# A decoder layer on one core: attention operands of 128 rows, values in 160 columns and loaded last, the norms' steps on GpSimd, and projection weights at the input's place modulo 512

## The chip, the core and the metric

The kernel runs on one core of a Trainium2 chip. The core has a matmul engine (TensorE, PE; its weight loads are listed apart as PEld), three engines for elementwise work (VectorE or DVE, ScalarE or ACT, GpSimd or POOL), and an engine that here only issues transfers (SyncE, SP). Each engine takes its instructions in order, and engines wait for one another by semaphores. Operands lie in on-chip memory, SBUF, as 128 rows (partitions), and an address below is the byte at which an operand starts within a row. The metric is the time of one execution on the device, in microseconds (us).

## The reference

One layer with batch 1, 2048 tokens, width 1024, in float32. Attention has 8 heads of 64 columns, the two other mixers 4 heads each.

```python
h = _rms(x, norm_mix_g);  z = h @ w_in + b_in       # columns split among three mixers
qa, ka = _rms(heads(a_q), a_q_g), _rms(heads(a_k), a_k_g)
c  = cumsum(log_sigmoid(a_f))                       # forget gate, one value per head and token
s  = qa @ ka^T * d**-0.5 + c[q] - c[k]              # causal, softmax over keys
ya = _rms(softmax(s) @ v, g_a)                      # normed per head of 64 columns
yb = sigmoid(b_o) * _rms(mlstm(silu(conv4(b_qk)), b_v, b_i, b_f), g_b)
yc = silu(c_g) * _rms(hgrn2(silu(c_q), logf, c_i), g_c)
x  = x + concat(ya, yb, yc) @ w_out
h  = _rms(x, norm_ffn_g)
u  = conv3(h @ w_up) + conv_b
x  = x + (silu(u_gate) * u_up) @ w_down
```

## The kernel before

**Precision.** A float32 operand is split into a high part (`hi`, rounded for the matmul engine's fp32r form) and a low part (`lo`, the rest). A product is three matmuls, hi by hi, hi by lo and lo by hi, all added into one accumulator: `mm3` (L193, its matmul is L198).

**Projection (z).** The normed input lies transposed in `hhi` and `hlo`, 16 KB a row for each half of the tokens. `z_groups` walks groups of columns of the weight. `load_split` (L178) brings the weights of a group in raw pieces, ACT makes `whi` (L188) and POOL `wlo` (L189). The *natural* groups have 256 or 264 weight columns, which the matmul streams against 128x128 pieces of the input; their result is drained by DVE with the bias added (`z<-w,bias`, L289). The groups for transposed results stream 512 columns of the input against weight pieces. Before the change `whi` starts at 192 or 448 modulo 512 (two buffers) and `hhi` at 64. The two other mixers run merged between the groups. Constants are cast at the start by `consts` (L1709) through one small buffer, `craw`: each load (L1715) waits for the cast before (L1716).

**Queries, keys, values** are written to the device's memory as they come out of the projection: `s_qh`, `s_ql`, `s_kh`, `s_kl` (L404) and `s_v` (L321), by POOL's queue, with the memsets (L315, L316) that complete a value tile.

**Attention.** For each head, `att_load` (L805) lets SP load two operand pairs. QA and KA (128 rows) hold high and low parts of queries and keys. QB and KB use 70 rows: 64 of queries and keys, and six with ones, maxima and gates, so that one matmul adds the gates and takes away the row maxima. V holds 16 blocks of 130 columns: 64 high values, a column for the sum, and 64 low values. Each head has two sets of tiles, used in turn.

The order is written out by hand. A head has 40 steps, one per block of 128 keys and up to 512 queries. A step issues the scores (L885 with KB and QB, L886 with KA and QA), ACT's exponential (L892) and its copy to the high part `ph` (L894), and the subtraction that makes the low part `pl` (L898): in three steps of four on POOL at once, in the fourth on DVE one step later. The row maxima of blocks further on are taken by another matmul (L845, `m<-KB,QB`) and a DVE maximum (L850), 12 of them before the first step. The values' three matmuls (L911, L912, L913; the last uses `pl`) follow the scores three steps behind. The loads of the next head stand early in a head (those of the first two before the first step).

`Later` is a list of functions to be called some steps on. Through it, `att_finish` (L937) norms a head in the next head's steps: squares on ACT, sums and the reciprocal root by Newton steps on DVE (`rms_steps`, L113: one start L120 to L122, and three rounds L130 to L132, one round a step), the scaling on DVE (L971), the gain on POOL (L976) and the store. The last head is finished in four quarters, one after each block of queries.

**After attention** come the output projection (`phase_out`, L198 again, with `wohi` and `yh`) and the feed-forward part (L1252, L1409). The functions that the diff touches, and what calls them:

## Time and profile before

| | before |
|---|---|
| median of 3 runs (lowest to highest) | 2932.36 us (2932.19 to 2941.21) |
| profiled execution, span | 2937.63 us, 2935.5 us |
| mean granted clock of TensorE | 0.977 |
| PE busy | 2817.4 us (96%) |
| DVE, POOL, ACT busy | 2005.9, 1435.1, 1280.0 us |
| projection with the two other mixers | 0 to 939 us |
| attention | 939 to 1443 us |
| output projection | 1443 to 1646 us |
| feed-forward | 1646 to 2935 us |

The profile is of one execution. Its page gives busy times and the costliest groups of instructions; the trace behind it also gives single instructions with their start. In such a row stand the start, the duration (both in us), the engine, the line, the operation with the tiles it writes and reads (out<-in) and their shapes, a count, and in brackets how long the engine was idle before it and what ended that. A window's row gives the busy time and count of each engine in a stretch of time, and the clock that TensorE was granted there, as a share of full speed. Matmuls overlap at their ends, so their spacing is read from start to start.

### The profile page before, as it was taken

Reading aid. Unit: us, or ns where it says so; the run is one execution under the profiler, and the core shown is the slowest. Engines: PE = TensorE matmul, PEld = TensorE weight load, DVE = VectorE, ACT = ScalarE, POOL = GpSimd, SP = SyncE. Lnnn points to the kernel's source line nnn. Section 1 sums busy time; section 2 is a strip of 40 time slices with the busy share of each in tenths; the row PEclk is TensorE's granted clock in tenths of the full one; section 3 lists DMA queues with packets and bytes.
Section 4 is the critical chain, followed back from the end, with each engine's and each line's share of the span. In section 5 each row is a group of like instructions: output and inputs, shape, how many; then the busy total and the mean of one; then the engine's idle time right before and its main releaser. Section 6 shows DMA issues by size and latency. Waiting matters only on the chain. (4 is left out here: it accounts for less than half of the span.)

```text
span 2935.5 us, 42833 instructions
## 1 busy us (share of the span) xinstructions
PE 2817.4 (96%) x15181; PEld 2342.7 (80%) x15181; DVE 2005.9 (68%) x3384; ACT 1280.0 (44%) x2167; POOL 1435.1 (49%) x1199
## 2 busy tenths in 40 slices
PE   7999988999988999999899899999999999999999
PEld 7898987889988666666688788888788888888887
DVE  7337687265786787778546577677797577777655
ACT  4213323132322778878424344444454343444443
POOL 2245452334454577766302366666475644444443
PEclk9999997999999999999999999999999999999999
DMA  4424434333334554342257444444777333333666
GB/s 159 127 93 133 150 96 143 94 108 97 111 107 143 107 114 88 81 92 49 72 179 246 148 155 151 154 148 158 268 247 271 114 108 108 108 105 117 232 214 209
DMA packets 346615, 411.07 MB, mean 140 GB/s; under 512 B 47650, under 2 KB 234096, under 8 KB 343232
## 3 DMA queue, kind: packets, MB, share of 16 engines
q1 hardware_dynamic: 292016, 318.45, 37.2%
q10 hardware_dynamic: 51952, 81.45, 7.6%
q0 software_dynamic: 2432, 8.42, 0.8%
q8 instruction: 120, 1.97, 0.3%
q14 instruction: 95, 0.78, 0.1%
HBM read 280.24 MB, written 127.98 MB: 139 GB/s over the span
## 5 line engine op out<-in xcount | busy, mean ns | idle before, releaser
L1221 POOL TENSOR_TENSOR w<-w,w 128x512 fp32r<-128x512 f32 x302 | 404.8, 1353 | 403.3 <-ACT w L1220 339.2
L1409 PE MATMUL ps<-w,w 128*128 128x512 f32 x1848 | 420.9, 389 | 4.0 <-ACT w L1400 2.0
L1409 PEld LDWEIGHTS ps<-w,w 128*128 128x128 f32 x1848 | 346.6, 188 | 77.6 <-ACT w L1400 2.4
L198 PE MATMUL w<-whi,hhi 128*128 128x256 f32 (+1 forms) x1280 | 370.4, 289 | 3.1 <-DVE lr L1766 2.0
L198 PE MATMUL w<-whi,hlo 128*128 128x256 f32 (+1 forms) x1280 | 371.3, 290 | 0.0
L198 PE MATMUL w<-wlo,hhi 128*128 128x256 f32 (+1 forms) x1280 | 370.4, 290 | 0.6 <-POOL wlo L189 0.6
L898 POOL TENSOR_TENSOR pl<-pf,ph 128x512 fp32r<-128x512 f32 (+2 forms) x240 | 287.8, 1212 | 146.6 <-ACT ph L894 133.3
L1402 POOL TENSOR_TENSOR w<-w,w 128x512 fp32r<-128x512 f32 x154 | 216.3, 1412 | 200.9 <-ACT w L1400 155.4
L1220 ACT ACTIVATE w<-w 128x512 fp32r<-128x512 f32 x302 | 180.4, 627 | 258.7 <-POOL w L1221 86.7
L850 DVE TENSOR_REDUCE mx<-m 128x1 f32<-128x512 f32 (+2 forms) x320 | 190.8, 605 | 91.3 <-PE m L845 63.1
L1401 DVE TENSOR_TENSOR w<-w,w 128x512 fp32r<-128x512 f32 x154 | 179.9, 1178 | 103.4 <-ACT w L1399 102.0
L198 PEld LDWEIGHTS w<-whi,hhi 128*128 128x128 f32 x1280 | 245.2, 192 | 4.8 <-issue 3.8
L198 PEld LDWEIGHTS w<-wlo,hhi 128*128 128x128 f32 x1280 | 244.9, 191 | 2.7 <-POOL wlo L189 1.0
L198 PEld LDWEIGHTS w<-whi,hlo 128*128 128x128 f32 x1280 | 244.7, 191 | 1.8 <-issue 0.5
L892 ACT ACTIVATE pf<-s 128x512 f32<-128x512 f32 (+1 forms) x320 | 172.5, 539 | 91.1 <-PE s L886 50.9
L1226 DVE TENSOR_TENSOR w<-w,w 128x512 f32<-128x512 f32 x176 | 149.8, 870 | 85.3 <-DMA w<-in_w_up_dram 81.0
L189 POOL TENSOR_TENSOR wlo<-wraw,whi 128x1024 fp32r<-128x1024 f32 (+1 forms) x56 | 135.3, 2433 | 111.7 <-ACT whi L188 102.2
L894 ACT ACTIVATE ph<-pf 128x512 fp32r<-128x512 f32 (+1 forms) x320 | 185.1, 578 | 10.3
L1267 DVE SCALAR_TENSOR_TENSOR u<-ps,fcol,u 128x1023 f32<-128x1023 f32 x88 | 108.9, 1279 | 95.3 <-ACT u L1266 95.3
L913 PE MATMUL pv<-pl,V 128*65 128x512 f32 (+1 forms) x320 | 121.7, 380 | 25.2 <-DVE pl L898 24.3
L1400 ACT ACTIVATE w<-w 128x512 fp32r<-128x512 f32 x154 | 96.6, 628 | 111.3 <-PE ps L1409 88.7
L1399 ACT ACTIVATE w<-w 128x512 fp32r<-128x512 f32 x154 | 95.9, 623 | 89.8 <-POOL w L1402 44.4
(374 smaller groups left out, 7092.1 us busy)
## 6 DMA issues: line engine op xcount, KB each, us to landing
w<-in_w_up_dram SPq DMA_DIRECT2D x182, 256.0 KB
w<-s_g SPq DMA_DIRECT2D x154, 256.0 KB
w<-in_w_down_dram SPq DMA_DIRECT2D x110, 256.0 KB
wraw<-in_w_in_dram SPq DMA_DIRECT2D x48, 512.0 KB
s_g<-u ACTq DMA_DIRECT2D x88, 256.0 KB
w<-s_w SPq DMA_DIRECT2D x88, 256.0 KB
s_g<-w ACTq DMA_DIRECT2D x66, 256.0 KB
x<-in_x_dram SPq DMA_DIRECT2D x32, 512.0 KB
```

The costliest lines, as they stand in the source:

```text
L189: nc.gpsimd.tensor_tensor(lo[:, q : q + n, :], raw, h.bitcast(F32), op=ALU.subtract)
L198: nc.tensor.matmul(out, lsl(lhs[a], i), rsl(rhs[b], i), start=(i == 0 and j == 0), stop=(i == n - 1 and j == 2))
L850: nc.vector.tensor_reduce(mx[:, i, kb : kb + 1], m[:, 0:n], axis=AX.X, op=ALU.max)
L892: nc.scalar.activation(pf[:, c0:], s[:, c0:], AF.Exp)
L894: nc.scalar.activation(ph[:, c0:], pf[:, c0:], AF.Copy)
L898: eng.tensor_tensor(pl[:, c0:], pf[:, c0:], ph[:, c0:].bitcast(F32), op=ALU.subtract)
L1220: nc.scalar.activation(h, t, AF.Copy)
L1221: nc.gpsimd.tensor_tensor(lo, t, h.bitcast(F32), op=ALU.subtract)
L1226: nc.vector.tensor_tensor(t, x, y, op=op)
L1401: nc.vector.tensor_tensor(gl, gr, gh.bitcast(F32), op=ALU.subtract)
L1402: nc.gpsimd.tensor_tensor(wl, wr, wh.bitcast(F32), op=ALU.subtract)
L1409: nc.tensor.matmul(tiles[tile], g[x][:, tile * P : (tile + 1) * P], w[y], start=j == 0 and c == 0, stop=j == nj - 1 and c == 2,)
```

## The change

1. `load_split` gives each weight tile 17 x 128 columns (8704 bytes, a multiple of 512) whatever its width, so both buffers start at 64 modulo 512, as the input does. A small pad tile goes, and two small tiles share a tag.
2. The casts of `consts` go through the three buffers of the tag `z`, which the projection's drains use too, in place of `craw`.
3. QB and KB become two fixed pairs of 128 rows. POOL zeroes rows 64 to 128 of both pairs once, before the first loads of ones and gates; L845 and L885 use all rows.
4. A row of V has 160 columns, and its low part begins at column 96. Each load of V is two transfers (65 and 64 columns), and all of V is loaded after the queries and keys.
5. In `att_finish`, the two scalings by the reciprocal sum, the three Newton rounds (four operations each in place of three) and the last scaling of the factor run on POOL; the start of the rounds stays on DVE. All heads share one tile of squares, and the last head's quarters are finished 18, 10, 4 and 4 steps after their last values in place of 4.

```diff
@@ -36,6 +36,8 @@
 NEG = -1e30
 
 SKEW, LEAD0, LEAD = 3, 12, 22
+
+VL, VW = 96, 160
 
 PLM = 4
 
@@ -110,7 +112,7 @@
         pass
 
 
-def rms_steps(k, pool, out, ss, n, epsf, tag):
+def rms_steps(k, pool, out, ss, n, epsf, tag, pool_too=False):
 
     nc = k.nc
     shp = list(ss.shape)
@@ -124,6 +126,12 @@
     )
     for _ in range(3):
         yield
+        if pool_too:
+            nc.gpsimd.tensor_tensor(u, out, out, op=ALU.mult)
+            nc.gpsimd.tensor_tensor(u, u, h, op=ALU.mult)
+            nc.gpsimd.tensor_scalar(out=u, in0=u, scalar1=1.5, scalar2=None, op0=ALU.add)
+            nc.gpsimd.tensor_tensor(out, out, u, op=ALU.mult)
+            continue
         if shp[1] == 1:
             nc.vector.scalar_tensor_tensor(u, out, h, out, op0=ALU.mult, op1=ALU.mult)
         else:
@@ -179,8 +187,11 @@
 
     nc = k.nc
     width = src.shape[1]
-    hi = k.t(wp, [P, DT, width], F32R, tag=tag + "hi")
-    lo = k.t(wp, [P, DT, width], F32R, tag=tag + "lo")
+
+    hi, lo = (
+        k.t(wp, [P, 17 * P], F32R, tag=tag + x)[:, 0 : DT * width].rearrange("p (n c) -> p n c", c=width)
+        for x in ("hi", "lo")
+    )
     for q in range(0, DT, n):
         raw = k.t(wp, [P, n, width], tag=tag + "raw")
         nc.sync.dma_start(raw, src[q * P : (q + n) * P, :].rearrange("(dt p) c -> p dt c", p=P))
@@ -214,7 +225,7 @@
 def z_stats(k, pz, xbufs):
 
     nc = k.nc
-    ss = k.t(pz, [P, 8], tag="n8s", bufs=1)
+    ss = k.t(pz, [P, 16], tag="ss")[:, 0:8]
     for b in range(2):
         for t in range(4):
             (x,) = z_load(k, 1, b, xbufs, t, 1)
@@ -805,8 +816,9 @@
 def att_load(k, h, st):
 
     r = slice(h * HD, (h + 1) * HD)
-    QA, KA, QB, KB = (k.t(k.pat[f"{t[1]}{h % 2}"], [P, T], F32R, tag=t) for t in ("QA", "KA", "QB", "KB"))
-    V = k.t(k.pat[f"V{h % 2}"], [P, 16, 130], F32R, tag="V")
+    QA, KA = (k.t(k.pat[f"A{h % 2}"], [P, T], F32R, tag=t) for t in ("QA", "KA"))
+    QB, KB = k.qkb[h % 2]
+    V = k.t(k.pat[f"V{h % 2}"], [P, 16, VW], F32R, tag="V")
     st.update(QA=QA, KA=KA, QB=QB, KB=KB, V=V, h=h)
 
     def ld(dst, src):
@@ -817,13 +829,14 @@
     ld(QB[64:70], k.s_one[0:6])
     ld(KB[64:68], k.s_one[6:10])
     ld(KB[68:70], k.s_fc[h])
-    v = k.s_v[:, h, :].rearrange("(jt p) c -> p jt c", p=P)
-    ld(V[:, 0:4], v[:, 0:4])
     ld(QA[0:64], k.s_qh[r])
     ld(QA[64:128], k.s_ql[r])
     ld(KA[0:64], k.s_kl[r])
     ld(KA[64:128], k.s_kh[r])
-    ld(V[:, 4:16], v[:, 4:16])
+    v = k.s_v[:, h, :].rearrange("(jt p) c -> p jt c", p=P)
+    for j in (slice(0, 4), slice(4, 16)):
+        ld(V[:, j, 0:65], v[:, j, 0:65])
+        ld(V[:, j, VL : VL + 64], v[:, j, 65:129])
 
 
 def att_maxima(k, sts, pa, ps, later):
@@ -843,7 +856,7 @@
                     nn = max(n, 256)
                     m = k.t(ps["m"], [P, BLK], tag="m")
                     nc.tensor.matmul(
-                        m[:, 0:nn], QB[0:70, q0 : q0 + P], KB[0:70, kb * BLK : kb * BLK + nn], start=True, stop=not last
+                        m[:, 0:nn], QB[:, q0 : q0 + P], KB[:, kb * BLK : kb * BLK + nn], start=True, stop=not last
                     )
                     if last:
                         nc.tensor.matmul(m[:, n - P : n], k.identb, k.mnat, start=False, stop=True)
@@ -882,7 +895,7 @@
     q0 = d * P
     qs = slice(qb * BLK + c0, (qb + 1) * BLK)
     s = k.t(ps["s"], [P, BLK], tag="s")
-    nc.tensor.matmul(s[:, c0:], KB[0:70, js], QB[0:70, qs], start=True, stop=False)
+    nc.tensor.matmul(s[:, c0:], KB[:, js], QB[:, qs], start=True, stop=False)
     nc.tensor.matmul(s[:, c0:], KA[:, js], QA[:, qs], start=False, stop=j < 4 * qb)
     if j >= 4 * qb:
         nc.tensor.matmul(s[:, q0 : q0 + P], k.identb, k.mtr, start=False, stop=d < 3)
@@ -909,7 +922,7 @@
     po = st["po"]
     nj = 4 * qb + 4
     nc.tensor.matmul(po[:, c0:], V[:, j, 0:65], ph[:, c0:], start=j == 0, stop=False)
-    nc.tensor.matmul(po[0:64, c0:], V[:, j, 65:129], ph[:, c0:], start=False, stop=False)
+    nc.tensor.matmul(po[0:64, c0:], V[:, j, VL : VL + 64], ph[:, c0:], start=False, stop=False)
     nc.tensor.matmul(po[:, c0:], V[:, j, 0:65], pl[:, c0:], start=False, stop=j == nj - 1)
     if j < nj - 1:
         return
@@ -929,7 +942,8 @@
 
     later.put(1, out)
     if h == AH - 1:
-        att_finish(k, st, pa, 4 * qb, 4, later, 4)
+
+        att_finish(k, st, pa, 4 * qb, 4, later, (18, 10, 4, 4)[qb])
     elif qb == 3:
         att_finish(k, st, pa, 0, 16, later, 4)
 
@@ -946,7 +960,9 @@
         o = st["o"][:, t0 : t0 + n, :]
         w["num"] = o[:, :, 0:64]
         w["rl"] = k.t(pa, [P, n], tag=f"rl{n}", bufs=bufs)
-        w["sq"] = k.t(pa, [P, n, HD], tag=f"asq{n}", bufs=bufs)
+        if n == 16 or "sq" not in st:
+            st["sq"] = k.t(pa, [P, 16, HD], tag="asq", bufs=1)
+        w["sq"] = st["sq"][:, t0 : t0 + n, :]
         w["ss"] = k.t(pa, [P, n], tag=f"ass{n}", bufs=bufs)
         nc.vector.reciprocal(w["rl"], o[:, :, 64])
 
@@ -957,17 +973,17 @@
         nc.vector.tensor_reduce(w["ss"][:, c], w["sq"][:, c], axis=AX.X, op=ALU.add)
 
     def scale():
-        nc.vector.tensor_tensor(w["ss"], w["ss"], w["rl"], op=ALU.mult)
-        nc.vector.tensor_tensor(w["ss"], w["ss"], w["rl"], op=ALU.mult)
+        nc.gpsimd.tensor_tensor(w["ss"], w["ss"], w["rl"], op=ALU.mult)
+        nc.gpsimd.tensor_tensor(w["ss"], w["ss"], w["rl"], op=ALU.mult)
         w["s"] = k.t(pa, [P, n], tag=f"as{n}", bufs=bufs)
-        w["chain"] = rms_steps(k, pa, w["s"], w["ss"], HD, 1.0, f"a{n}")
+        w["chain"] = rms_steps(k, pa, w["s"], w["ss"], HD, 1.0, f"a{n}", pool_too=True)
 
     def link():
         next(w["chain"], None)
 
     def times(c):
         if c.start == 0:
-            nc.vector.tensor_tensor(w["s"], w["s"], w["rl"], op=ALU.mult)
+            nc.gpsimd.tensor_tensor(w["s"], w["s"], w["rl"], op=ALU.mult)
         nc.vector.tensor_tensor(
             w["sq"][:, c], w["num"][:, c], w["s"][:, c].unsqueeze(2).broadcast_to([P, 4, HD]), op=ALU.mult
         )
@@ -1003,8 +1019,16 @@
 
     sts = [{} for _ in range(AH)]
     later = Later()
+
+    k.qkb = [[k.t(k.pat[f"B{i}"], [P, T], F32R, tag=t) for t in ("QB", "KB")] for i in range(2)]
+    def zero(i):
+        for x in k.qkb[i]:
+            k.nc.gpsimd.memset(x[64:128].bitcast(F32), 0.0)
+
+    zero(0)
     with k.tc.manual_schedule():
         att_load(k, 0, sts[0])
+        zero(1)
         att_load(k, 1, sts[1])
         mx = att_maxima(k, sts, pa, ps, later)
         for _ in range(LEAD0):
@@ -1586,7 +1610,6 @@
             for _ in z_norm(k, 0, 0, pz, psw, xb):
                 pass
             z = z_groups(k, 0, pz, wp, psw, xb)
-            pz.tile([P, 24], F32, tag="padz", name="padz", bufs=1)
             state(k, mconst)
             for _ in range(ZC):
                 next(z)
@@ -1711,7 +1734,7 @@
     nc = k.nc
 
     def cast(dst, src):
-        raw = cm.tile([P, P], F32, tag="craw", name=k.nm("craw"))[:, 0 : src.shape[1]]
+        raw = k.t(pz, [P, P], tag="z", bufs=3)[:, 0 : src.shape[1]]
         nc.sync.dma_start(raw, src)
         nc.vector.tensor_copy(dst, raw)
```

The order of the instructions moves at three places. First POOL's queue at the end of the projection and the start of attention, before the change, from the completion of the last value tile (`h`) on:

```order
L318 TENSOR_TENSOR h_9610<-z_9553,h_9610 128x4x64
L321 DMA s_v<-h_9604 128x520
L321 DMA s_v<-h_9610 128x520
L898 TENSOR_TENSOR pl_9787<-pf_9783,ph_9785 128x512
L898 TENSOR_TENSOR pl_9805<-pf_9801,ph_9803 128x384
```

And with the change:

```order
L332 DMA s_v<-h_9603 128x520
L332 DMA s_v<-h_9609 128x520
L1026 MEMSET QB_9689 64x2048
L1026 MEMSET KB_9690 64x2048
L1026 MEMSET QB_9691 64x2048
L1026 MEMSET KB_9692 64x2048
L911 TENSOR_TENSOR pl_9794<-pf_9790,ph_9792 128x512
```

The four zeroings come after the last store of values and before the first low part of the probabilities.

Second, SP's queue where it loads a head's operands (shown for the third head; each head is loaded in the same order), before:

```order
L813 DMA QB_10554<-s_one 6x2048
L813 DMA KB_10555<-s_one 4x2048
L813 DMA KB_10555<-s_fc 2x2048
L813 DMA V_10556<-s_v 128x4x130
L813 DMA QA_10552<-s_qh 64x2048
L813 DMA QA_10552<-s_ql 64x2048
L813 DMA KA_10553<-s_kl 64x2048
L813 DMA KA_10553<-s_kh 64x2048
L813 DMA V_10556<-s_v 128x12x130
```

And with the change:

```order
L825 DMA QB_9689<-s_one 6x2048
L825 DMA KB_9690<-s_one 4x2048
L825 DMA KB_9690<-s_fc 2x2048
L825 DMA QA_10559<-s_qh 64x2048
L825 DMA QA_10559<-s_ql 64x2048
L825 DMA KA_10560<-s_kl 64x2048
L825 DMA KA_10560<-s_kh 64x2048
L825 DMA V_10561<-s_v 128x4x65
L825 DMA V_10561<-s_v 128x4x64
L825 DMA V_10561<-s_v 128x12x65
L825 DMA V_10561<-s_v 128x12x64
```

The values move behind the queries and keys. For the first head the loads of ones (`QB<-s_one`, `KB<-s_one`) wait for POOL's zeroings, and the rows behind them are issued after them.

Third, POOL's queue in the middle of attention, where a head is finished, with the change (`as` is the factor of the norm, `a16u` a scratch tile, `rl` the reciprocal sum; before, POOL had only the `pl` rows here):

```order
L911 TENSOR_TENSOR pl_10790<-pf_10786,ph_10788 128x512
L130 TENSOR_TENSOR a16u_10759<-as_1723_10756 128x16
L131 TENSOR_TENSOR a16u_10759<-a16u_10759,a16h_10758 128x16
L132 TENSOR_SCALAR a16u_10759<-a16u_10759 128x16
L133 TENSOR_TENSOR as_1723_10756<-as_1723_10756,a16u_10759 128x16
L911 TENSOR_TENSOR pl_10810<-pf_10806,ph_10808 128x512
L130 TENSOR_TENSOR a16u_10759<-as_1723_10756 128x16
L131 TENSOR_TENSOR a16u_10759<-a16u_10759,a16h_10758 128x16
L132 TENSOR_SCALAR a16u_10759<-a16u_10759 128x16
L133 TENSOR_TENSOR as_1723_10756<-as_1723_10756,a16u_10759 128x16
L986 TENSOR_TENSOR as_1723_10756<-as_1723_10756,rl_1690_10650 128x16
L911 TENSOR_TENSOR pl_10848<-pf_10844,ph_10846 128x512
```

The rounds stand between the low parts, in the order of the steps that call them.

## The prediction

> **What bounds the kernel now.** I read the page first, then busy time and clock by stage, then the groups of matmuls by form, and last the rows around the places that the change touches. The stages are the projection (0 to 939 us), attention (to about 1443), the output projection (to 1646) and the feed-forward part (to the end).
>
> ```profile
> PE 2817.4 (96%) x15181; PEld 2342.7 (80%) x15181; DVE 2005.9 (68%) x3384; ACT 1280.0 (44%) x2167; POOL 1435.1 (49%) x1199
> ...
> 940.00:960.00 20.00, 11.92 (x38) 7.67 (x39) 11.44 (x27) 4.59 (x10) 8.53 (x18) 0.58 0.90 259
> 960.00:1400.00 440.00, 419.56 (x2188) 287.14 (x2187) 342.79 (x661) 351.35 (x665) 303.80 (x260) 0.96 0.43 86
> 1400.00:1450.00 50.00, 43.31 (x190) 30.03 (x189) 31.00 (x78) 27.05 (x52) 27.20 (x26) 0.86 0.15 43
> ...
> 1646.00:2935.50 1289.50, 1267.69 (x5561) 1042.26 (x5558) 923.44 (x1084) 559.46 (x884) 705.27 (x519) 1.00 0.52 169
> ```
>
> The columns of a window are its length, then busy time and count of PE, PEld, DVE, ACT and POOL, the granted clock, the DMA share and GB/s. TensorE is the bound nearly everywhere. So an edit pays in one of three ways: a matmul takes less time, an idle stretch of PE goes, or the clock stays up. Every idle stretch costs twice, since the clock is low behind it: 0.58 at attention's start, 0.96 within it, 0.86 at its end. In the feed-forward part, which the change leaves alone, there is nothing to win.
>
> **The change part by part.** *Operand addresses in the projection.* The rows give the spacing of matmuls from start to start, at full clock.
>
> ```profile
> 82.39 0.40 PE L198 MATMUL w<-hlo,whi 128*128 128x512 f32 x1
> ...
> 90.79 0.40 PE L198 MATMUL w<-hlo,whi 128*128 128x512 f32 x1
> 918.95 0.28 PE L198 MATMUL w<-whi,hhi 128*128 128x256 f32 x1
> ...
> 936.87 0.28 PE L198 MATMUL w<-wlo,hhi 128*128 128x256 f32 x1
> ...
> 1800.42 0.39 PE L1252 MATMUL ps<-b21l,w 128*128 128x512 f32 x1
> ...
> 1908.09 0.39 PE L1252 MATMUL ps<-t2h,w 128*128 128x512 f32 x1
> ```
>
> Between the first two rows lie 36 matmuls of 512 columns: 8.40 us / 36 = 233.3 ns each. Between the last two lie 477: 107.67 / 477 = 225.7 ns. In the feed-forward part both operands start at the same place modulo 512 bytes (448); in the projection the input starts at 64 and the weights at 192 or 448, which the change makes 64. Taken as the cause, that is 7.6 ns on the 768 matmuls of this form (256 of each of three groups): -5.8 us. It is the only difference between the two streams that I see, so I take -5, with bounds 0 and -6.
>
> For the narrower ones, the middle pair gives 17.92 us / 151 = 118.7 ns per 256 columns. Half of the feed-forward spacing is 112.9. If the whole time shrinks in proportion, 3072 matmuls gain 5.8 ns each, -18 us, and the 768 of 264 columns about -3 more. If there is a fixed part per matmul, 118.7 may already be the full rate and the gain is 0. The bounds are 0 and -21. I take -5, nearer to nothing, because a fixed part is what the groups below suggest: their mean records do not halve either (291 ns for 256 columns, 402 for 512).
>
> ```profile
> L198 PE MATMUL w<-whi,hlo 128*128 128x256 f32 x1024 | 297.9, 291 | 0.0
> ...
> L198 PE MATMUL w<-hhi,whi 128*128 128x512 f32 x256 | 102.3, 402 | 0.3 <-ACT hhi L174 0.3
> ...
> L845 PE MATMUL m<-KB,QB 70*128 70x512 f32 x224 | 100.0, 451 | 1.7 <-DVE mx L850 1.5
> L885 PE MATMUL s<-QB,KB 70*128 70x512 f32 x224 | 96.1, 429 | 0.0
> ...
> L886 PE MATMUL s<-QA,KA 128*128 128x512 f32 x224 | 92.1, 411 | 6.1 <-DMA KA<-s_kh 6.1
> ```
>
> The Trainium skill, TensorE: Matmul & The Clock Gate, section "Back-to-back issue gap", gives a warm gap of 262 cycles for 256 columns and 518 for 512, so 106.7 ns between them at its 2.4 GHz; 225.7 less that is 119.0, and by that rule the term of -5 would be 0 and the sum 5 us higher. The trace's 118.7 agrees with it.
>
> *Operands of 128 rows, values at 640 bytes a row.* In attention the six full-width kinds run at this spacing:
>
> ```profile
> 1230.09 0.39 PE L913 MATMUL pv<-pl,V 128*65 128x512 f32 x1
> 1230.32 0.40 PE L885 MATMUL s<-QB,KB 70*128 70x512 f32 x1
> 1230.56 0.40 PE L886 MATMUL s<-QA,KA 128*128 128x512 f32 x1
> 1230.79 0.39 PE L845 MATMUL m<-KB,QB 70*128 70x512 f32 x1
> ```
>
> That is 0.70 us / 3 = 233 ns, against 225.7 in the feed-forward part. The two kinds with 70 rows have the longest means of all (451 and 429 ns), but they also follow the bf16 masks and the transposes, and the spacing behind L886, which has 128 rows already, is no shorter. The trace holds no attention matmul with all conditions that the change makes, so both ends stay: 0, if rows and addresses count for nothing here, and 1344 x 7.6 ns = -10 us with about -1 for the 384-wide ones. The stream that is nearest to the changed one, all rows used and all starts on a round place, is the feed-forward one; I take -11. The Trainium skill, TensorE: Matmul & The Clock Gate, section "LDWEIGHTS (loading the stationary operand)", speaks against this: a load's time goes with its columns and not with its rows. By it the term would be 0 and the sum 11 us higher; the trace cannot tell, since the loads here are covered by matmuls.
>
> *The norms' steps on GpSimd.* Each head has one stall of PE, behind a low part that DVE makes late:
>
> ```profile
> L913 PE MATMUL pv<-pl,V 128*65 128x512 f32 (+1 forms) x320 | 121.7, 380 | 25.2 <-DVE pl L898 24.3
> ...
> 1210.12 0.18 DVE L132 SCALAR_TENSOR_TENSOR as<-a16u,as 128x16 f32<-128x16 f32 x1
> ...
> 1211.85 1.22 DVE L131 TENSOR_TENSOR a16u<-a16u,a16h 128x16 f32<-128x16 f32 x1
> ...
> 1215.94 0.81 DVE L970 TENSOR_TENSOR as<-as,rl 128x16 f32<-128x16 f32 x1
> ...
> 1218.22 1.74 DVE L898 TENSOR_TENSOR pl<-pf,ph 128x512 fp32r<-128x512 f32 x1
> ...
> 1217.29 0.73 POOL L976 TENSOR_TENSOR asq<-asq,ga 128x256 f32<-128x256 f32 x1 [0.57 <-DVE asq L971]
> ...
> 1220.51 1.27 POOL L898 TENSOR_TENSOR pl<-pf,ph 128x512 fp32r<-128x512 f32 x1
> ...
> 1220.02 0.69 PE L913 MATMUL pv<-pl,V 128*65 128x512 f32 x1 [2.36 <-DVE pl L898]
> ```
>
> A step of 16 columns takes DVE 0.18 us alone and up to 1.22 while POOL is in a long operation. DVE then waits for the norm before it may scale, and the pl behind that (1218.22) is late. The eleven steps that go free about 5 us of DVE per head. But the norm still has to come, now from 15 small POOL operations queued between POOL's own pl. Price: POOL takes 0.73 us for 256 columns and 1.27 for 512, so 2.1 ns a column over 0.19; an estimate for 16 columns is 0.22, and 0.22 to 0.30 with a gap between dependent ones. At 0.26 the last step waits behind one pl (1.27) and needs 5 x 0.26 = 1.3: 2.6 us, against 1214.85 to 1216.75 and the wait before it now. That is about even. Each 0.08 us off in the pitch moves the norm by 13 x 0.08 = 1 us a head, and the clock doubles it. The stalls behind these pl sum to 24.3 us, and the low clock of attention (0.96 over 440 us) costs 0.04 x 440 = 17 to 18. Bounds: +10 (pitch 0.35 and more, POOL's own pl late too) and -12 (norm 0.75 us earlier in each head, with the clock). I take -3, for the freed DVE.
>
> *Zeroed rows at attention's start, values last.* Rows 64 to 128 of the first operands must be zeroed before the ones are loaded over them. In the new order the four zeroings stand on POOL behind the last store of the values, and SP's loads of the ones wait for them, with all the queries, keys and values queued behind.
>
> ```profile
> 916.81 0.52 SPq L813 DMA_DIRECT2D QB<-s_qh  x1
> ...
> 938.95 0.19 PEld L845 LDWEIGHTS m<-KB,QB 70*128 70x128 f32 x1
> ...
> 941.45 0.85 SPq L813 DMA_DIRECT2D KA<-s_kh  x1
> ...
> 951.89 1.11 POOL L321 DMA_DIRECT2D s_v<-h  x2
> ...
> 953.71 0.79 PE L886 MATMUL s<-QA,KA 128*128 128x512 f32 x1 [6.11 <-DMA KA<-s_kh]
> ...
> 0.74 0.95 POOL L1578 MEMSET q<- 128x1024 f32 x1 [0.29 <-POOLq L1807]
> ```
>
> Now the maxima start at 938.95, the keys are asked for at 941.45, and the first full scores come at 953.71, 12 us after the request, 6.1 of them stalled. After the change POOL reaches the zeroings when the last stores are issued: 953.0 now, some 4 to 6 us earlier without the loads that compete with the stores (DMA share 0.90 here), so 947 to 949. A zeroing of 1024 columns took 0.95 us, so about 1.9 for 2048; the two that gate are done at 951 to 953. The ones, queries and keys follow: requests until about 956, four loads of 0.5 MB at the 259 GB/s of this window in 8 us, scores at about 964, the values a little later. That is +10 us. The bounds are +5 (stores far earlier) and +14 (no earlier at all). The stall of 6.1 us that values loaded last could take away is inside: the keys are then ahead of the values, but everything is behind the zeroing.
>
> *Constants through three shared buffers.* The nine casts at the start lose their own buffer and now stand on DVE in a row just ahead of a drain.
>
> ```profile
> 73.24 0.41 DVE L289 TENSOR_TENSOR z<-w,bias 128x256 f32<-128x256 f32 x1
> ...
> 73.87 0.36 PE L198 MATMUL w<-whi,hhi 128*128 128x264 f32 x1 [2.00 <-DVE lr L1766]
> ...
> 45.18 0.36 PE L198 MATMUL w<-whi,hhi 128*128 128x264 f32 x1 [1.06 <-DVE cmask L1716]
> ```
>
> PE already waits 2.00 us here. I read the casts (about 0.2 us each) and their loads as pushing this drain to about 77 or 78: +4 to +5, less the stall of 1.06 us that a cast causes now at 45.18. I take +3, bounds 0 and +8.
>
> *The last head's finish* has two chains in POOL's queue at once, and the first output matmuls come later in PE's order. Now the tail's last stalls are short:
>
> ```profile
> 1440.84 0.47 PE L925 MATMUL x<-ident,oT 65*128 65x65 f32 x4 [0.68 <-ACT oT L919]
> ...
> 1443.63 0.79 PE L198 MATMUL w<-wohi,yh 128*128 128x512 f32 x1 [0.69 <-ACT yh L1088]
> ```
>
> Two chains of 15 steps at 0.26 us are 7.8 us of POOL, mostly beside the last steps' matmuls. I take +2, with bounds -3 (the freed DVE) and +10 (all of it in the open, with the clock).
>
> *Value loads* in two pieces double their packets, in a stage whose DMA share is 0.43; the next head's loads are asked for some 16 steps ahead. Cost 0; without that cover a late V would cost a few us per head.
>
> **Sum:** -5 - 5 - 11 - 3 + 10 + 3 + 2 = -9 us. The profiled execution took 2937.63 us for a span of 2935.5, so the same execution would take 2928.6. The runs shown have a median of 2932.36, 5 us lower; from there it is **2923 us**, right at 0.3% (9 us), which is about what a measurement of this kernel can tell from no change.
>
> **Rivals.** (1) *The zeroing decides: slower.* PE waits from 939 to about 954 for the first operands; if the matmuls keep their spacing (no gain of 21), the start's +10 to +14 stands alone with +3 and +2: 2932 + 15 - 3 = 2944, up to 2952. For it: the order on SP and POOL, and L886 at 233 ns with 128 rows. Against it: the feed-forward spacing. It decides as soon as the start costs over 9 us more than the matmuls gain. (2) *The stall per head goes.* If the freed DVE makes its pl in time, up to 24.3 us of stalls and part of the 17 us of clock go: some -30 beyond the -3, 2893. For it: 5 us of DVE per head freed where the queue is full (10 steps in 14 us). Against it: DVE still waits for the norm. (3) *POOL becomes late.* Three of four steps give POOL a pl of 1.27 us and four small operations of 1.0, together 2.3, where a step lasts about 1.41; over four steps it falls 1.8 us behind and the POOL pl stalls PE in place of the DVE one: with the clock +20, 2943. Against it: POOL is 69% busy and values follow three steps behind. (4) *The addresses do nothing and the rest cancels:* the change doesn't do what it says, 2932 to 2940.
>
> **How the numbers follow.** The forecast has 0.44, the rivals 0.16, 0.14, 0.10 and 0.16. The forecast's own range is 2908 to 2938, by the unknown spacing (0 to -38 in all) and the start; with the rivals, 2895 to 2948. Faster by over 0.3%: 0.28 of the first and all of (2), 0.42. Within: 0.15, and 0.11 of (4), 0.04 of (1) and (3): 0.30. Slower: 0.28.
>
> **What would show it.** Spacing of 226 ns in place of 233 in the 512-wide projection matmuls, and in L885, L886 and the three value matmuls; a spacing still at 233 in attention fells the largest gain. The 256-wide ones at 117 would bear out -5; 118.7 says 0. First maxima matmul at about 954, first full scores at 964. The stall per head at L913 still about 2.5 us and behind DVE; behind POOL, rival (3); gone, rival (2). The drain at 73.24 moved to about 77. The prediction is wrong above all if the clock in attention moves away from 0.96, which no single row here sets.

## The result, and the profile after

The changed kernel took 2971.09 us (median of 4 runs, 2968.34 to 2973.06), against 2936.6 us (median of 4, 2932.19 to 2941.21) for the kernel before in runs beside it. The ratio is 1.0123, with a 95% interval of 1.0106 to 1.0141: slower by 36 us. The forecast was 2923 us, with a range of 2895 to 2948. The profiled execution has a span of 2971.3 us, 35.8 more than before.

By the marks that PE's rows give, the time came in like this (us):

| stretch | before | after | difference |
|---|---|---|---|
| start to the last projection matmul | 938.9 | 948.4 | +9.5 |
| from there to the first value matmul | 21.5 | 29.4 | +7.9 |
| first to last value matmul | 479.4 | 498.0 | +18.6 |
| last value matmul to the first feed-forward matmul | 206.8 | 204.1 | -2.6 |
| from there to the end of the span (its program is the same) | 1288.9 | 1291.3 | +2.4 |

Of the 18.6 us between the first and the last value matmul, half fall in the first seven heads (416.6 to 425.9 us) and half in the last one (62.9 to 72.2), counted from its first value matmul.

The windows of the changed kernel show the same places; columns are as before (length, busy time and count of PE, PEld, DVE, ACT, POOL, clock, DMA share, GB/s).

```profile
0.00:87.00 87.00, 64.17 (x469) 62.20 (x470) 56.50 (x145) 33.55 (x50) 18.49 (x22) 0.96 0.49 154
...
950.00:980.00 30.00, 15.98 (x56) 10.10 (x57) 12.96 (x29) 5.66 (x13) 15.26 (x21) 0.60 0.86 198
980.00:1420.00 440.00, 409.27 (x2159) 279.07 (x2158) 311.25 (x559) 345.96 (x655) 320.12 (x354) 0.97 0.42 84
1420.00:1480.00 60.00, 45.26 (x193) 28.74 (x192) 20.58 (x44) 31.00 (x59) 41.24 (x83) 0.83 0.10 27
```

DVE is busy 311 us of 440 in place of 343, POOL 320 in place of 304, and PE has lost 10 us of busy time. The idle times of PE say why. First the groups of the changed kernel (busy time and mean, then the idle time before them and who ended it), then single rows of its trace.

```profile
L926 PE MATMUL pv<-pl,V 128*65 128x512 f32 (+1 forms) x320 | 122.9, 384 | 42.6 <-DVE pl L911 34.1
L858 PE MATMUL m<-KB,QB 128*128 128x512 f32 (+2 forms) x320 | 131.8, 420 | 14.1 <-DMA KB<-s_fc 13.3
```

```profile
79.48 0.56 PE L209 MATMUL w<-whi,hhi 128*128 128x264 f32 x1 [8.87 <-DVE pg L305]
...
961.97 0.55 PE L858 MATMUL m<-KB,QB 128*128 128x256 f32 x1 [13.27 <-DMA KB<-s_fc]
...
971.93 0.77 PE L899 MATMUL s<-QA,KA 128*128 128x512 f32 x1 [1.77 <-DMA KA<-s_kh]
...
1239.65 0.45 PE L926 MATMUL pv<-pl,V 128*65 128x512 f32 x1 [0.64 <-POOL pl L911]
...
1245.34 0.44 PE L926 MATMUL pv<-pl,V 128*65 128x512 f32 x1 [3.81 <-DVE pl L911]
```

Three waits have grown. The early one, behind the casts, is 8.87 us, where 2.00 and 1.06 stood. A new one of 13.27 us stands at attention's first matmul, of which 4.3 us come back at L899 (1.77 in place of 6.11). And the stalls at the values' third matmul (waits of PE within attention) sum to 42.6 us in place of 25.2.

### The profile page after: what moved, and what is told of

Same layout as the page of the kernel before. It is cut to its first block, busy times and chain, and to the rows that moved or that the text cites. A ratio compares the mean times of both kernels' runs of the same rounds, so it can differ in the third digit from the quotient of the medians.

```text
span 2971.3 us, 42898 instructions
## 1 busy us (share of the span) xinstructions
PE 2819.4 (95%) x15181; PEld 2343.6 (79%) x15181; DVE 1955.7 (66%) x3252; ACT 1279.6 (43%) x2167; POOL 1477.8 (50%) x1368
## 5 line engine op out<-in xcount | busy, mean ns | idle before, releaser
L1245 POOL TENSOR_TENSOR w<-w,w 128x512 fp32r<-128x512 f32 x302 | 406.5, 1359 | 401.7 <-ACT w L1244 278.9
L1244 ACT ACTIVATE w<-w 128x512 fp32r<-128x512 f32 x302 | 180.4, 627 | 258.8 <-POOL w L1245 89.6
L926 PE MATMUL pv<-pl,V 128*65 128x512 f32 (+1 forms) x320 | 122.9, 384 | 42.6 <-DVE pl L911 34.1
L858 PE MATMUL m<-KB,QB 128*128 128x512 f32 (+2 forms) x320 | 131.8, 420 | 14.1 <-DMA KB<-s_fc 13.3
L1424 ACT ACTIVATE w<-w 128x512 fp32r<-128x512 f32 x154 | 96.7, 628 | 111.9 <-PE ps L1433 89.0
```

Source lines behind the costliest of these rows:

```text
L1244: nc.scalar.activation(h, t, AF.Copy)
L1245: nc.gpsimd.tensor_tensor(lo, t, h.bitcast(F32), op=ALU.subtract)
```

## The experiments

Twelve kernels were run. All ratios are to the kernel before on the same chip; 0.001 is about 2.9 us. The theory was that the loss sits in the three waits, each of one edit. The rival was that it sits in the new tiles themselves.

**Undo one edit of the changed kernel.** *The rows.* L858 and L898 use 70 rows again, and nothing is zeroed.

```diff
-    nc.tensor.matmul(s[:, c0:], KB[:, js], QB[:, qs], start=True, stop=False)
+    nc.tensor.matmul(s[:, c0:], KB[0:70, js], QB[0:70, qs], start=True, stop=False)
-    zero(0)
-        zero(1)
```

> The change with 70 rows again in the first operand pair and no zeroing; all else as changed. Theory (the time went into three waits: casts, zeroing, norm steps on GpSimd): the wait of 13.3 us for KB<-s_fc at attention's start goes, and the first full scores follow the projection by about 12 us less; 10 to 16 us faster than the change, so about 2955 to 2961. Rival (the new tiles themselves, padded or 160 wide, slow what reads and loads them): within 4 us of the change, 2967 to 2975. If the 128 rows shorten the score matmuls, this kernel loses 2 to 5 us of its gain in the body of attention.

Measured: 1.0081 (1.0066 to 1.0096), so 12 us less than the change. The first maxima came 0.1 us after the projection, in place of 13.6, and the first full scores 8.4 us after it, in place of 23.5. From the first to the last value matmul it took 501.0 us, 3 us more than the change. Both are as the theory had them.

*The casts.* They go through the two buffers of another tag that is free at that time.

```diff
-        raw = k.t(pz, [P, P], tag="z", bufs=3)[:, 0 : src.shape[1]]
+        raw = k.t(pz, [P, D], tag="x", bufs=2)[:, 0 : src.shape[1]]
```

> The change with the nine casts of the constants through the two buffers of the tag x, which nothing else uses at that time, in place of the three that the drains use. Theory: PE's wait of 8.87 us at 79.5 us goes back to about 2, the rest stays: 6 to 9 us faster than the change, 2962 to 2965. Rival (that wait is only shifted to the next place, since the loads are behind it in SP's queue): 0 to 2 us faster.

Measured: 1.0079 (1.0064 to 1.0094), 13 us less than the change. PE's wait is 1.95 us at 72.56, and the projection ends at 939.1 in place of 948.4. The gain is larger than the 6 to 9 us that were expected, and than the wait.

*The norms.* The scalings, the three rounds and the last factor are on DVE again.

```diff
-        w["chain"] = rms_steps(k, pa, w["s"], w["ss"], HD, 1.0, f"a{n}", pool_too=True)
+        w["chain"] = rms_steps(k, pa, w["s"], w["ss"], HD, 1.0, f"a{n}")
-            nc.gpsimd.tensor_tensor(w["s"], w["s"], w["rl"], op=ALU.mult)
+            nc.vector.tensor_tensor(w["s"], w["s"], w["rl"], op=ALU.mult)
```

> The change with the norms' steps on DVE again, as before the change (three operations a round). Theory: the stalls at L926, 3.7 to 4.0 us and 0.6 to 1.0 us in each head, go back to about 2.8 in one, and the four waits of 0.9 to 3.5 us of the last head shrink: 14 to 22 us faster than the change, 2949 to 2957. Rival (the stalls come from the values in 160 columns and twice as many packets, or from the freed order of DVE): the stalls stay and the time is within 5 us of the change.

Measured: 1.0026 (1.0015 to 1.0037), 28 us less than the change, more than expected. First to last value matmul: 471.9 us, against 498.0 with the change and 479.4 before it. The first seven heads are 17.6 us shorter than in the change, and the last one 8.7 us. The groups of this kernel at L926, by form:

```profile
L926 PE MATMUL pv<-pl,V 128*65 128x512 f32 x224 | 91.0, 406 | 21.3 <-DVE pl L911 21.1
...
L926 PE MATMUL pv<-pl,V 128*65 128x256 f32 x64 | 18.6, 291 | 7.6 <-DVE pl L911 7.6
```

That is 28.9 us of stalls, against 42.6 in the change and 25.2 before it.

*All three.* What is left is the padded weights, the new values, their place in the queue and the last head's later finish.

The three diffs above, in one kernel.

> The change with all three of these undone: what is left is the padded weight tiles, the values in 160 columns, loaded last in two pieces, the shared tile of squares and the last head's later finish. Theory: 33 to 42 us faster than the change, so no slower than the kernel before, 2929 to 2938. Rival (some of the loss sits in what is left): 2945 and more.

Measured: 0.997 (0.9956 to 0.9984), faster than before by 9 us. So no loss is left in the rest, and the rival is out. The single savings sum to 53 us where all together give 45; with intervals of some 4 us each way on every one of these ratios, the two are not told apart.

**Do one edit alone, on the kernel before.** *The norms on GpSimd*, with the last head finished as before:

```diff
-        w["chain"] = rms_steps(k, pa, w["s"], w["ss"], HD, 1.0, f"a{n}")
+        w["chain"] = rms_steps(k, pa, w["s"], w["ss"], HD, 1.0, f"a{n}", pool_too=True)
-            nc.vector.tensor_tensor(w["s"], w["s"], w["rl"], op=ALU.mult)
+            nc.gpsimd.tensor_tensor(w["s"], w["s"], w["rl"], op=ALU.mult)
```

> The kernel before with one edit: the scalings and the three rounds of the norms on GpSimd (the last head's too, finished 4 steps after its values as before). Theory: the loss is in this edit by itself, 20 to 30 us, 1.007 to 1.010 of the kernel before, with stalls at L913 of 3.5 us or more in each head. Rival (it costs only beside the new tiles and the last head's later finish): 1.003 or less.

Measured: 1.0084 (1.0067 to 1.0101). The edit costs 25 us by itself, as the theory had it. Against the kernel before, the first seven heads are 14.2 us longer and the last one 12.3 us. Its groups at L919, which is L913 of before:

```profile
L919 PE MATMUL pv<-pl,V 128*65 128x512 f32 x224 | 93.9, 419 | 36.0 <-DVE pl L904 32.5 <-POOL pl L904 3.5
...
L919 PE MATMUL pv<-pl,V 128*65 128x256 f32 x64 | 18.7, 293 | 7.9 <-DVE pl L904 7.9
```

*The casts through the drains' buffers:*

```diff
-        raw = cm.tile([P, P], F32, tag="craw", name=k.nm("craw"))[:, 0 : src.shape[1]]
+        raw = k.t(pz, [P, P], tag="z", bufs=3)[:, 0 : src.shape[1]]
```

> The kernel before with one edit: the nine casts through the three buffers of the tag z. Theory: PE waits 8 to 10 us at about 80 us in place of 2.0 and 1.1, and the projection ends 7 to 10 us later; 1.002 to 1.0035 of the kernel before. Rival (it only cost beside the padded tiles): 1.001 or less.

Measured: 1.0044 (1.0027 to 1.0061), 13 us, more than expected. This row is PE's wait, and the window is that of the same kernel:

```profile
79.77 0.56 PE L198 MATMUL w<-whi,hhi 128*128 128x264 f32 x1 [8.96 <-DVE pg L294]
...
80.00:90.00 10.00, 10.00 (x51) 8.90 (x52) 1.38 (x7) 2.41 (x3) 4.34 (x2) 0.84 0.30 78
```

The wait is 6 us longer than the two that it replaces, and the clock in the 10 us behind it is 0.84; in the four kernels with this edit it was 0.75 to 0.87 there, and 1.00 in all the others. The projection ends at 952.4, 13.5 us later than before. Some 6 us of that are longer waits of PE in the merged mixers after 90 us, and these are not shown to come from the casts: the kernel with the norms' edit alone, whose program is the same up to attention, waits 4 us longer there too and ends the projection at 943.5. In the four kernels with the casts' edit the projection ends at 947 to 952, and in the five without it and without loaded zeros at 938 to 944.

*Both loads of the values behind those of queries and keys:*

```diff
-    v = k.s_v[:, h, :].rearrange("(jt p) c -> p jt c", p=P)
-    ld(V[:, 0:4], v[:, 0:4])
     ld(QA[0:64], k.s_qh[r])
     ...
     ld(KA[64:128], k.s_kh[r])
+    v = k.s_v[:, h, :].rearrange("(jt p) c -> p jt c", p=P)
+    ld(V[:, 0:4], v[:, 0:4])
     ld(V[:, 4:16], v[:, 4:16])
```

> The kernel before with one edit: both loads of the values behind those of queries and keys. Theory: the wait of 6.1 us for KA at L886 falls to under 2 us and no wait at the first L911 takes its place; 4 to 8 us faster, 0.997 to 0.9985 of the kernel before. Rival (the values are then late): the wait moves to L911 and the time is that of before.

Measured: 0.9974 (0.9963 to 0.9985), 8 us faster, as the theory had it. Its first full scores and first values:

```profile
948.01 0.63 PE L886 MATMUL s<-QA,KA 128*128 128x512 f32 x1
...
954.57 0.63 PE L911 MATMUL pv<-ph,V 128*65 128x512 f32 x1
```

No wait is left at either; before, they stood at 953.71 (after 6.11 us) and 960.43.

**Other ways to the 128 rows.** The next kernels have the norms on DVE and the casts undone, and take the zeros from memory instead of POOL. First 58 rows of zeros:

```diff
+    if h < 2:
+        ld(QB[70:128], k.s_zero)
+        ld(KB[70:128], k.s_zero)
```

> The change with the norms' steps on DVE, the casts through the tag x, and the zeros of rows 70 to 128 loaded from memory (58 rows, early in SP's queue) in place of POOL's zeroing. Theory: the wait for KB<-s_fc was only POOL's lateness, so the first maxima come right after the projection (under 1 us of wait) and the 128 rows keep their spacing of about 230 to 232 ns in L858 and L898 against 235; 3 to 8 us faster than the kernel with 70 rows and all three undone, so 0.994 to 0.996 of the kernel before. Rival: the 1.9 MB of zeros delay the queries and keys behind them, and the start gives back what the rows bring: 0.997 or more.

Measured: 1.0078 (1.0057 to 1.0099), against the theory. Most of the reason is in these rows: the zeros were asked for at 928, and the first maxima came 40 us later. The window is of the same kernel, inside that wait.

```profile
927.87 0.70 SPq L825 DMA_DIRECT2D QB<-s_zero  x1
928.90 0.24 SPq L825 DMA_DIRECT2D KB<-s_zero  x1
...
967.77 0.55 PE L861 MATMUL m<-KB,QB 128*128 128x256 f32 x1 [19.70 <-issue]
...
953.00:957.00 4.00, 0.00 (x0) 0.00 (x0) 0.00 (x0) 0.42 (x1) 1.00 (x4) 0.50 0.12 51
```

By the trace these 19.70 us are a wait for the zeros, although the row says "issue". In the window the DMA share is 0.12, about two of the core's 16 DMA engines, at 51 GB/s. The projection itself ends at 947.8 in this kernel, 10 us later than with all three edits undone; where that comes from was not followed.

Then all of rows 64 to 128, loaded before the ones go over them, and the narrow weight tiles at 192 modulo 512:

```diff
+    if h < 2:
+        ld(QB[64:128], k.s_zero)
+        ld(KB[64:128], k.s_zero)
     ld(QB[64:70], k.s_one[0:6])
```

> The change with the norms' steps on DVE, the casts through the tag x, the 256 and 264 wide weight tiles at 192 modulo 512, and zeros loaded from memory over all of rows 64 to 128 (64 rows in place of 58), before the ones are loaded over them. Theory (the load of 58 rows was slow by its shape, 40 us from issue to the first maxima, and neither zeros as such nor the rows cost time): the wait of 19.7 us at attention's start falls to 2 us or less, the 7.2 us wait at 1010 goes too, and what the rows (3 to 7 us) and the narrow tiles (3 to 4 us) bring shows: 0.993 to 0.996 of the kernel before. Rival (zeros from memory delay what is behind them in any shape): 0.998 or more.

Measured: 0.9975 (0.9964 to 0.9985), between what was expected (0.993 to 0.996) and the rival (0.998), and no faster than the kernel with 70 rows and all three edits undone (0.997). The first maxima come at 942.29, 0.1 us after the projection, and the wait at 1010 is gone. While the zeros were loaded, the DMA engines were all busy:

```profile
926.00:934.00 8.00, 8.00 (x70) 8.00 (x69) 7.49 (x23) 1.26 (x2) 0.79 (x1) 1.00 1.00 208
```

The zeros now stand ahead of the ones in SP's queue, and their shape differs; the two were not tried apart. From the first to the last value matmul it takes 472.6 us. A wait of 3.73 us at the second block of scores is new; it ended with ACT, whose copy `ph` waited, by the trace, for a store of values. So the first value matmul comes 19.0 us after the projection, where the kernel with all three undone has 15.0.

The narrow tiles at 192 were also tried beside the first form of the zeros:

```diff
-        k.t(wp, [P, 17 * P], F32R, tag=tag + x)[:, 0 : DT * width].rearrange("p (n c) -> p n c", c=width)
+        k.t(wp, [P, 17 * P], F32R, tag=tag + x)[:, o : o + DT * width].rearrange("p (n c) -> p n c", c=width)
...
-        w = load_split(k, wp, w_in[:, off : off + width], n=4)
+        w = load_split(k, wp, w_in[:, off : off + width], n=4, o=32)
```

The second pair is in the 256 and 264 wide groups; for the 512 wide ones `o` stays 0.

> As the kernel with loaded zeros, but the weight tiles of the 256 and 264 wide groups begin 128 bytes further on (192 modulo 512, the input at 64), while those of the 512 wide groups stay at 64. Theory (equal places help the wide matmuls and hurt the narrow ones): the 256-wide spacing goes from 119.4 back to 118.3 ns and the 512-wide stays at 227 to 228; 3 to 4 us less in the projection, which a whole time may not show. Rival (the 1.2 ns have another cause): the spacing stays at 119.4.

Measured: 1.0076 (1.005 to 1.0101) against 1.0078 without it; a whole time does not show it. The spacing does. First the changed kernel, with both kinds at 64, then this one:

```profile
89.08 0.40 PE L209 MATMUL w<-hhi,whi 128*128 128x512 f32 x1
...
124.90 0.39 PE L209 MATMUL w<-hhi,wlo 128*128 128x512 f32 x1
...
928.23 0.28 PE L209 MATMUL w<-whi,hhi 128*128 128x256 f32 x1
...
946.34 0.29 PE L209 MATMUL w<-wlo,hhi 128*128 128x256 f32 x1
```

```profile
81.42 0.39 PE L209 MATMUL w<-hlo,whi 128*128 128x512 f32 x1
...
117.03 0.39 PE L209 MATMUL w<-hhi,wlo 128*128 128x512 f32 x1
...
927.13 0.28 PE L209 MATMUL w<-whi,hhi 128*128 128x256 f32 x1
...
945.05 0.28 PE L209 MATMUL w<-wlo,hhi 128*128 128x256 f32 x1
```

In the changed kernel, 158 wide matmuls take 35.82 us, 226.7 ns each, and 151 narrow ones 18.11 us, 119.9 each. With the narrow tiles at 192 it is 157 in 35.61, 226.8, and 151 in 17.92, 118.7. Before, it was 233.3 and 118.7. So equal places modulo 512 take 6.6 ns off the wide matmuls and put 1.2 ns on the narrow ones. Over all gaps between wide matmuls of the projection the middle values are 232 ns before and 227 after, so 5 ns.

**What POOL's queue does to the norm.** Rounds on GpSimd, two steps apart, in the kernel with 58 loaded rows (`i` is the step at which the next round is called):

```diff
-        i += 1
+        i += 2 if n == 16 else 1
```

> As the kernel with loaded zeros, but with the norms' steps of the first seven heads on GpSimd, one round every two steps in place of one every step (the last head's on DVE). Theory (the change lost here because a low part and four small operations, 2.4 us, are more than a step of 1.4 us, so POOL fell behind): POOL keeps up, the stalls at L926 fall from 3.8 and 0.6 us in a head to under 1 in all, and the body of attention is 8 to 20 us shorter than with the steps on DVE. Rival (what costs is that DVE waits for POOL at all, and that POOL's reads hold up DVE's): the stalls stay at 2 us or more in a head and the time is that of the kernel with the steps on DVE or above.

Measured: 1.0094 (1.0079 to 1.0109), not told apart from the same kernel with the steps on DVE (1.0078). DVE's wait for the factor fell only from 3.7 to 5.9 us in a head (4.5 on average, in the change) to 1.6 to 5.0 (3.1 on average): the factor stands behind a low part on POOL, and DVE asks in the same step. PE's stalls stay at 2.9 us or more in each of these heads, as the rival had it. So the theory, that the pace alone was at fault, does not hold. Last, in the kernel with 64 loaded rows, rounds every step, but DVE asks four steps later; `factor` is the last product by `rl`, on POOL, and DVE's scalings come after the second line:

```diff
+    later.put(i, factor)
+    i += 4 if n == 16 else 0
```

> As the kernel with 64 loaded rows, but with the norms of the first seven heads on GpSimd, one round a step, and DVE's scalings four steps later than the last round, so that DVE does not wait for them. Theory (the change lost here because DVE asked for the factor 4.6 us before POOL had it): DVE's waits for POOL's factor go from 4.6 us to under 0.5, the stalls at L926 fall to under 1.5 us a head, and with DVE free of the eleven steps the body is 5 to 20 us shorter than with the steps on DVE. Rival (POOL's own low parts are late behind the small operations, or the DVE low part is late from the scalings alone): stalls of 2 us or more stay in each head and the time is within 4 us of the kernel with the steps on DVE, or above.

Measured: 0.995 (0.9935 to 0.9965), the fastest kernel here, 2925.9 us where the kernel before had 2941.83 on that chip. DVE no longer waits for the factor, and the two largest groups at L929 (the same matmul) hold 20.0 us of stalls:

```profile
L929 PE MATMUL pv<-pl,V 128*65 128x512 f32 x224 | 90.1, 402 | 13.4 <-POOL pl L914 9.6 <-DVE pl L914 3.7
...
L929 PE MATMUL pv<-pl,V 128*65 128x256 f32 x64 | 18.6, 291 | 6.6 <-DVE pl L914 5.8 <-POOL pl L914 0.8
```

The expectation is met in part. Stalls of 2.2 to 2.9 us in all stay in each of the heads two to seven, where under 1.5 was expected, and about half of them now end with POOL, as the rival had it; but the time is 7 us below the kernel with 64 loaded rows, which differs only in the norms, where the rival allowed 4. Against that kernel the first seven heads take 401.7 us in place of 411.0, and the last one 66.4 in place of 61.6. In the seven heads PE is idle for 15.2 us in place of 19.7; the rest of the gain goes with the clock. The first window is of the kernel with 64 loaded rows, the second of this one:

```profile
1000.00:1394.00 394.00, 373.88 (x1992) 255.41 (x1990) 313.42 (x599) 321.38 (x611) 285.06 (x244) 0.98 0.42 85
```

```profile
1000.00:1385.00 385.00, 369.20 (x1992) 250.78 (x1991) 284.14 (x515) 321.69 (x611) 308.56 (x347) 1.00 0.43 87
```

Between them the stalls differ in length: single ones of up to 2.9 us there, none over 1.2 us here.

## Why the prediction was wrong

**The norms' steps: the step that failed.** The prediction took -3, bounds -12 and +10; alone they cost 25 us. The price of one operation was about right: mostly 0.21 to 0.25 us, 0.28 to 0.35 from start to start (0.22, and 0.22 to 0.30, forecast). The error is in "At 0.26 the last step waits behind one pl (1.27) and needs 5 x 0.26 = 1.3: 2.6 us" and in the "about even" that follows from it. That counts the last round only. These rows of the changed kernel show the rounds in POOL's queue and what waits for them:

```profile
1235.94 1.30 POOL L911 TENSOR_TENSOR pl<-pf,ph 128x512 fp32r<-128x512 f32 x1
...
1237.19 0.22 POOL L130 TENSOR_TENSOR a16u<-as 128x16 f32<-128x16 f32 x1
...
1238.14 0.22 POOL L133 TENSOR_TENSOR as<-as,a16u 128x16 f32<-128x16 f32 x1
1238.32 1.28 POOL L911 TENSOR_TENSOR pl<-pf,ph 128x512 fp32r<-128x512 f32 x1
...
1240.80 0.22 POOL L986 TENSOR_TENSOR as<-as,rl 128x16 f32<-128x16 f32 x1
...
1241.05 1.48 DVE L987 TENSOR_TENSOR asq<-ao,as 128x256 f32<-128x256 f32 x1 [4.63 <-POOL as L986]
...
1243.54 1.74 DVE L911 TENSOR_TENSOR pl<-pf,ph 128x512 fp32r<-128x512 f32 x1
```

A low part and a round take 1238.32 - 1235.94 = 2.38 us, where a step takes some 1.4, so each round comes about 1 us later than the step that calls it. DVE, in order, stands still 4.63 us with a maximum and its own low part behind it. The edit frees about 5 us of DVE per head, and 4.63 of them DVE spends waiting. The third rival had the sum (2.3 us where a step lasts 1.41) and +20 us, but put the stall on POOL's low part and got 0.10; most of it was DVE's. (Its 1.8 us over four steps does not follow from its own numbers: three low parts and four rounds are 7.8 us where four steps last 5.6, so 2.2.)

The prediction also priced the last head's finish apart, at +2, with bounds -3 and +10. The last head took 9.3 us more, half of the loss within attention, and the cause is the same queue, at an end where two quarters are finished at once:

```profile
1455.50 0.76 DVE L987 TENSOR_TENSOR asq<-ao,as 128x256 f32<-128x256 f32 x2 [9.25 <-POOL as L986]
```

DVE waits 9.25 us for the factor there. The stalls of the finish at L926 are 7.8 us, in four rows of 0.86 to 3.54, where two of 4.01 and 0.66 stood before, and the clock of that window is 0.83. The later finish by itself is not at fault: the kernel with the norms on DVE keeps it, and its last head takes 63.5 us.

The second rival, that the stall goes with a freed DVE, did not come true in the change; where DVE asks late enough, the stalls fall from 26.8 us (64 loaded rows, norms on DVE) to 20.7, not to nothing.

**The casts: right mechanism, term too small.** +3, bounds 0 and +8; the projection ended 9.5 us later, and alone the edit cost 13.

```profile
77.62 0.73 DVE L1739 CAST cmask<-z 128x64 uint8<-128x64 f32 x3 [2.41 <-DMA z<-in_cmask_dram]
...
78.84 0.42 DVE L300 TENSOR_TENSOR z<-w,bias 128x256 f32<-128x256 f32 x1
...
80.00:90.00 10.00, 10.00 (x54) 8.87 (x52) 1.55 (x7) 2.63 (x4) 4.76 (x3) 0.87 0.35 99
```

The drain came at 78.84, where 77 or 78 was worked out, because the casts wait for their loads one after another, and PE's wait grew by 5.8 us. Left out was the low clock behind it (0.87 from 80 to 90 us, where the kernel before had 1.00), though the prediction itself says that an idle stretch costs twice; that is some 1.3 us. What makes up the rest of the 9.5 and 13 us is open, since the projection's end also moves by 6 us between kernels that have neither this edit nor loaded zeros.

**The zeroing: right.** +10, bounds +5 and +14, with the gain of the values loaded last inside; from the projection to the first value matmul it took 7.9 us more, and undoing the zeroing gave 12. A zeroing took 1.80 us (estimate 1.9); the first maxima came 13.6 us after the projection (15 forecast) and the first scores 23.5 (25). POOL reached the zeroings 7.2 us after the projection's end (8 to 10 forecast).

```profile
954.48 1.11 POOL L332 DMA_DIRECT2D s_v<-h  x2
955.62 1.80 POOL L1026 MEMSET QB<- 64x2048 f32 x1
957.37 1.80 POOL L1026 MEMSET KB<- 64x2048 f32 x1
...
959.19 0.26 SPq L825 DMA_DIRECT2D KB<-s_one  x1
...
961.57 0.59 SPq L825 DMA_DIRECT2D KA<-s_kh  x1
```

The first rival rested on this place and was the right side, but not for its reason alone: it took the start for the whole loss, where undoing it gave a third.

**Addresses: -5 right for the wide, wrong sign for the narrow.** 768 x 6.6 ns = -5.1 us as forecast (-3.8 with the 5 ns of all gaps). The feed-forward spacing that it was taken from is 226.7 ns and not 225.7, for between its two rows lie 475 matmuls and not 477; 226.7 is what the wide matmuls reached. For the narrow ones -5 was taken; each took 1.2 ns more, +3.7 us over 3072. The Trainium skill, TensorE: Matmul & The Clock Gate, section "Back-to-back issue gap", has 256 cycles between the gaps of 256 and 512 columns, 106.7 ns at its 2.4 GHz, which gives an estimate of 120.0 for the narrow ones with the right count. The trace agrees after the change, 226.7 - 119.9 = 106.8 ns; before it the difference was 233.3 - 118.7 = 114.6.

**128 rows and aligned values: -11, too large.** Undisturbed spacing at full clock went from 235.1 (153 intervals) to 232.5 ns (154) at L898, from 234.8 to 230.1 at L858, from 235.1 to 232.2 at L899 and from about 232.3 to 231.5 at the values: 3 us in all, and not down to the spacing of the feed-forward part. With all three edits undone, and so 70 rows, it is 235.0 at L898 and 235.7 at L858. By the Trainium skill, TensorE: Matmul & The Clock Gate, section "LDWEIGHTS (loading the stationary operand)", a weight load takes no longer with more rows, and the term would be 0. The spacing here even fell a little with the rows; why is open.

**Values last: hidden in a term.** The prediction saw the 6.1 us and put it "inside" the zeroing's +10. Alone the order of the loads is worth 8 us, the only gain among the three edits that were tried alone.

## What to carry to other kernels

A step moved to a less busy engine does not come free of that engine's queue: add up the queue's work per period over all the steps moved, not the last one, and ask when the old engine will want the result; if it must wait in order, move the asking later with it. Price a stall of the matmul engine with the low clock behind it, and look at the length of single stalls and not only at their sum. A change of many small edits is worth taking apart: here one edit of five (values loaded last) was worth 8 us and three others hid it.

## What the runs showed that was not expected

**The length of a stall and the clock.** In the 14 profiles, between 40 us after the first value matmul and 36 us before the last, none of the 32 idle stretches of PE of 0.9 to 1.7 us had a lower clock in it or in the 6 us behind it, 45 of 62 of 2.2 to 3.2 us had, and all 28 longer ones. So the stalls of some 2.5 us in the kernel before cost clock in most heads, those of 3.7 us in the change in all, and the short ones of the fastest kernel in none of the first seven heads.

**Rows and the clock.** With the same kind of stalls, this profile of the kernel before, with 70 rows in the first pair, was granted less clock in the body of attention than that of the change with its norms on DVE, with 128. The first row is the kernel before.

```profile
961.00:1400.00 439.00, 418.56 (x2186) 286.56 (x2185) 341.82 (x659) 350.83 (x663) 303.80 (x260) 0.97 0.43 86
```

```profile
977.00:1400.00 423.00, 402.01 (x2161) 275.14 (x2161) 338.75 (x638) 345.13 (x654) 302.72 (x258) 0.99 0.45 88
```

That is 439 / 2186 = 200.8 ns per matmul against 423 / 2161 = 195.7. That the rows do this is not shown. Of the stalls of 2.2 to 3.2 us, 27 of 28 cost clock with 70 rows and 18 of 34 with 128, but 6 of 7 did in the kernel with 58 loaded rows, which also has 128, and with the stalls of 3.7 us and more all did in both. These are single profiles; over all executions the mean clock is 0.977 to 0.982 both for the kernel with 64 loaded rows (12 executions) and for the one with 70 rows and all three edits undone (7), and their times are 0.9975 and 0.997. So no gain of the rows is seen in the whole time.

**58 rows or 64.** Loads of 58 rows of 8 KB behind the ones held attention up by some 20 us, loads of 64 rows ahead of them not at the first maxima. The two windows above show a DMA share of 0.12 at the tail of the one and of 1.00 during the other, so the smaller load used far fewer of the DMA engines at its end; whether its place in the queue added to that is not shown.

**Places modulo 512** act with opposite sign on 512 and 256 columns, -6.6 and +1.2 ns. The cause is open.
